# A tuned fp32 transformer trunk on one core: weight sums queued one split later, transposes moved behind the next block's first product, one filler step moved to the end of a block

## The chip, the cores and the metric

The kernel runs on one core of a Trainium2 chip. Its time is the device time of the whole program in microseconds; the time before is the median of three runs. All instructions are written out in a flat program without loops on the chip. A scheduler orders each engine's queue when the program is built: every instruction has the priority of its place in the traced Python code, and an instruction of lower priority is put first where the one ahead of it is not ready by the scheduler's own estimate. At run time each engine works through its queue strictly in order and waits on semaphores.

## The reference, cut to what matters

Two layers over x of 256 rows by 2048 columns, all in float32. Layer 0 has a gated linear attention mixer and layer 1 a sparse attention mixer; the change touches neither. After each mixer comes the same feed-forward part, with D_FF = 5632:

```
def swiglu(h, w1, w3, w2):
    return (jax.nn.silu(h @ w1) * (h @ w3)) @ w2
...
        x = x + y
        x = x + swiglu(rmsnorm(x, norm_ffn[i]), ffn_w1[i], ffn_w3[i], ffn_w2[i])
```

## The kernel before

**Split weights.** TensorE works on a reduced-precision form of float32, so each operand is split in two. A weight tile of 512 x 512 (1 MB, as 128 partitions x 2048 elements) is loaded by DMA, ScalarE casts it to its high part `wh` (L136), and VectorE subtracts to get the low part `wl` (L137). Each product is then three matmuls: high x high, high x low, low x high. Both `wh` and `wl` have three buffers, so a split can begin only when TensorE has finished with the tile that was split three splits earlier. Tiles that arrive for one use only go to four `raw` buffers.

**Blocks.** `ffn` (L561) goes over D_FF in units of 512 columns. `plain` does unit 0. Then come seven blocks per layer (L594), fourteen in all. Each block computes its own unit of `h @ w1` and `h @ w3` together in `pair` (L369), as a 2 x 2 block product done with seven products in place of eight. Below they are p1 to p7, by their forms A11, F5, F3, A12, F6, F7, N22; each takes two weight tiles and 24 matmuls. The seven products need sums of weight tiles:

- `va` and `vb` are loaded into fixed homes, `vc` and `vd` into `raw` buffers.
- p1 uses `va`; right after each of its two splits VectorE adds `vb` to that half of `va` (`plus`, L405, the instruction at L406). p2 uses the sum.
- After p2's splits the GpSimd queue starts a DMA that adds a tile from memory to `va` (`plus_dma`, L408 and L409). The second half's DMA is issued when the first half's has landed. p5 uses the result.
- p3 uses `vc`, and VectorE adds `vc` to `vb` (L406 again). A `raw` buffer of `vc` is free for its next load when this sum is done. p6 uses `vb`.
- After p5's splits two more DMAs of L409 add a tile to `va`, again one after the other; p7 uses that.

**Filler steps.** Wherever `pair` yields, `ffn` runs one step of other work: eight steps to a block, s0 to s7, each with one `raw` weight tile and 24 matmuls. In four of the seven blocks of a layer the work is `pieces` (L538), the down projection of two finished units: its matmuls are L551 to L553, its tile in PSUM is `down`, and after every second step VectorE adds two PSUM tiles to x (L558). In the first, the fourth and the last block it is `plain_steps` (L477), a further unit of `h @ w1` and `h @ w3` (matmuls L494, tile `half`). The order on TensorE is

```
p1 s0 p2 s1 p3 s2 p4 s3 p5 s4 p6 s5 s6 p7 s7 | p1 s0 ...
```

**Transposes.** When a block's unit is done it has to be transposed and split (`split_t`, L209, or `turned` in `plain_steps`, L515): eight transposes on TensorE, two casts on ScalarE (L218 or L528), two subtractions on VectorE (L219 or L529). These are generators in the deque `side`; `tick` (L116) runs one step of the first of them, and a product or a filler step ticks after every second of its k tiles. So they fall into p1 of the next block; behind a block with `plain_steps` there are two units to turn, and they fill p1 wholly.

Of the kernel before, what the change touches and what calls it, by code (L numbers as in the profile page):

```python
# [55 lines left out]
def trunk(  # L56
# [7 lines left out]
    nc = tc.nc  # L64
# [47 lines left out]


    side = deque()

    def tick():  # L116

        while side:
            try:
                return next(side[0])  # L120
            except StopIteration:
                side.popleft()
# [9 lines left out]
    def split_w(raw, pool=wp):  # L132

        wh = pool.tile([P, 4, NB], F32R, tag="wh", bufs=3 if pool is wp else 1, name="wh")
        wl = pool.tile([P, 4, NB], F32R, tag="wl", bufs=3 if pool is wp else 1, name="wl")
        nc.scalar.copy(wh, raw)  # L136
        nc.vector.tensor_sub(wl, raw, wh.bitcast(F32))  # L137
        return wh, wl

    def gemm_tail(w, c0, parts, pool, done):  # L140
# [228 lines left out]
    def pair(nrm, wa, wb, c0, turn, done):  # L369

        def src(w, j, c):
            r = j * 1024 + c * 512
            return w[r:r + 512, c0:c0 + NB].rearrange("(k p) n -> p k n", p=P)

        def load(w, j, homes):
            o = []
            for c, (pool, tag, bufs) in enumerate(homes):
                raw = pool.tile([P, 4, NB], F32, tag=tag, bufs=bufs, name=tag)  # L380
                nc.sync.dma_start(raw, src(w, j, c))
                o.append(raw)
            return o

        def product(acc, raws, form, start, stop, then=None):
            for c in range(2):
                wh, wl = split_w(raws[c])
                if then is not None:
                    then(c)
                hi, lo = nrm.forms[form]  # L390
                for j in range(4):
                    k = 4 * c + j
                    for i, (l_, r_) in enumerate(((hi, wh), (hi, wl), (lo, wh))):
                        nc.tensor.matmul(acc, l_[:, k, :], r_[:, j, :], start=start and k == i == 0,  # L394
                                         stop=stop and k == 7 and i == 2, skip_group_check=not start)
                    if j % 2:
                        tick()

        def bank():
            return acc_p.tile([P, NB], F32, tag="acc", name="acc")  # L400

        def sums(tag):
            return nrm.pool.tile([P, NB], F32, tag=tag, bufs=1, name=tag)

        def plus(dst, other):  # L405
            return lambda c: nc.vector.tensor_add(dst[c], dst[c], other[c])  # L406

        def plus_dma(dst, w, j):  # L408
            return lambda c: nc.gpsimd.dma_start(dst[c], src(w, j, c), accum_op=ALU.add)  # L409

        fz = nrm.pool
        stream = [(wp, "raw", RAW)] * 2
        homes = [((fz, "v0", 1), (fz, "v1", 1)), ((fz, "v2", 1), (res, "g3", 1))]
        va = load(wa, 0, homes[turn])
        vb = load(wb, 0, homes[1 - turn])
        b1 = bank()
        product(b1, va, "A11", True, True, plus(va, vb))
        s1 = sums("s1")
        nc.scalar.copy(s1, b1)
        yield  # L420
        b2 = bank()
        product(b2, va, "F5", True, True, plus_dma(va, wb, 1))
        y = sums("y")
        nc.vector.tensor_sub(y, b2, s1)
        yield
        vc = load(wb, 1, stream)
        product(b2, vc, "F3", False, True, plus(vb, vc))
        yield
        vd = load(wa, 1, stream)
        product(b1, vd, "A12", False, True)  # L430
        done("11", b1)
        yield
        b3 = bank()
        product(b3, va, "F6", True, True, plus_dma(va, wa, 1))
        w = sums("w")
        nc.vector.tensor_sub(w, b3, s1)
        nc.vector.tensor_add(w, w, b2)
        done("12", w)
        yield
        product(b3, vb, "F7", False, True)  # L440
        nc.vector.tensor_add(y, y, b3)
        yield
        yield
        product(b3, va, "N22", False, True)
        nc.vector.tensor_sub(s1, s1, b3)
        done("21", s1)
        done("22", y)
        yield

    def plain(nrm, ws, c0, done):  # L450
# [26 lines left out]
    def plain_steps(ws, b, forms, sc, ready):  # L477

        flat = res.tile([P, 4 * NB], F32, tag=f"g{b % 3}", name="early")
        us = [flat[:, t * NB:(t + 1) * NB] for t in range(NT)]  # L480
        s1 = flat[:, NT * NB:(NT + 1) * NB]
        for q, w in enumerate(ws):
            acc = [ms_p.tile([P, NB], F32, tag="ms", name="half") for _ in range(2)]
            for gi in range(4):
                raw = wp.tile([P, 4, NB], F32, tag="raw", bufs=RAW, name="raw")
                nc.sync.dma_start(raw, w[gi * NB:(gi + 1) * NB, b * NB:(b + 1) * NB].rearrange("(k p) n -> p k n", p=P))
                wh, wl = split_w(raw)
                for bank, form, start, stop in ((0, "A11", True, True), (1, "F7", True, True)) if gi < 2 else \
                        ((0, "A12", False, True), (1, "N22", True, True)):
                    hi, lo = forms[form]  # L490
                    for j in range(4):
                        k = 4 * (gi % 2) + j
                        for i, (l_, r_) in enumerate(((hi, wh), (hi, wl), (lo, wh))):
                            nc.tensor.matmul(acc[bank], l_[:, k, :], r_[:, j, :], start=start and k == i == 0,  # L494
                                             stop=stop and k == 7 and i == 2, skip_group_check=not start)
                        if j % 2:
                            tick()
                if gi == 1:
                    nc.scalar.copy(s1, acc[0])
                    nc.vector.tensor_add(s1, s1, acc[1])  # L500
                    acc[1] = ms_p.tile([P, NB], F32, tag="ms", name="half")
                if gi < 3:
                    yield
            r = sc["r"]
            if q == 0:
                nc.scalar.activation(us[0], acc[0], AF.Silu, scale=r[:, 0:1])
                nc.vector.tensor_sub(s1, s1, acc[1])
                nc.scalar.activation(us[1], s1, AF.Silu, scale=r[:, 1:2])
                yield
            else:  # L510
                nc.vector.scalar_tensor_tensor(us[0], us[0], r[:, 0:1], acc[0], op0=ALU.mult, op1=ALU.mult)
                nc.vector.tensor_sub(s1, s1, acc[1])
                nc.vector.scalar_tensor_tensor(us[1], us[1], r[:, 1:2], s1, op0=ALU.mult, op1=ALU.mult)

        def turned():  # L515
            tr = []
            for kk in range(2):
                tr.append(tr_p.tile([P, 2, SEQ], F32, tag="tr", name="tr"))
                for t in range(NT):
                    for k in range(2):  # L520
                        c = (2 * kk + k) * P
                        nc.tensor.transpose(tr[kk][:, k, t * P:(t + 1) * P], us[t][:, c:c + P], ident)
                if kk == 0:
                    yield
            hi, lo = hi_lo(b % 3)
            for kk in range(2):
                sl = slice(2 * kk, 2 * kk + 2)
                nc.scalar.copy(hi[:, sl, :], tr[kk])  # L528
                nc.vector.tensor_sub(lo[:, sl, :], tr[kk], hi[:, sl, :].bitcast(F32))  # L529
            part[:2] = hi, lo  # L530
            ready.add(b * NB)
            yield

        part = [None, None, b * NB]
        side.append(turned())
        yield part

    def pieces(w, parts):  # L538

# [21 lines left out]
    def ffn(layer, nrm):  # L561
# [2 lines left out]
        sc = {}  # L564
        parts = []
        ready = set()

        def block(b, us):
            def turned():
                yield from split_t(us, hi, lo)  # L570
                ready.add(b * NB)

            hi, lo = hi_lo(b % 3)
            side.append(turned())
            parts.append((hi, lo, b * NB))

        def gate(us):
# [16 lines left out]
        for turn, (b, inner) in enumerate(((2, 1), (3, None), (4, None), (6, 5), (7, None), (8, None), (10, 9))):  # L594
# [5 lines left out]
            us = [None] * NT  # L600
            made = None
            for slot, _ in enumerate(pair(nrm, w1, w3, b * NB, 1 - turn % 2, gate(us))):
                if inner is None and slot == 0:
                    assert all(r0 in ready for _, _, r0 in two)
                made = next(work)
            if inner is not None:
                parts.append(made)
            block(b, us)
        return w2, parts


# [554 lines left out]
```

## Time and profile before

| | us |
|---|---|
| median of 3 runs | 2260.61 (2259.99 to 2260.88) |
| profiled execution, its own time | 2262.72 |
| its span, first to last instruction | 2260.9 |
| TensorE busy | 2226.0 (98%) |
| VectorE busy | 1576.4 (70%) |
| ScalarE busy | 1169.4 (52%) |
| mean granted TensorE clock | 0.999 |

PE is TensorE, PEld its weight load, DVE VectorE, ACT ScalarE, POOL GpSimd and SPq the DMA queue of SyncE. TensorE's busy time counts pipelined matmuls, whose records overlap by 0.16 us: the starts of two matmuls with 512 columns are 0.23 us apart, while one record lasts 0.39 us. So an idle time that is shown is shorter than the delay between starts.

### The profile page before, as it was taken

Reading aid. Unit: us, or ns where it says so; the run is one execution under the profiler, and the core shown is the slowest. Engines: PE = TensorE matmul, PEld = TensorE weight load, DVE = VectorE, ACT = ScalarE, POOL = GpSimd, SP = SyncE. Lnnn points to the kernel's source line nnn. Section 1 sums busy time; section 2 is a strip of 40 time slices with the busy share of each in tenths; the row PEclk is TensorE's granted clock in tenths of the full one; section 3 lists DMA queues with packets and bytes.
Section 4 is the critical chain, followed back from the end, with each engine's and each line's share of the span. In section 5 each row is a group of like instructions: output and inputs, shape, how many; then the busy total and the mean of one; then the engine's idle time right before and its main releaser. Section 6 shows DMA issues by size and latency. Waiting matters only on the chain.

```text
span 2260.9 us, 25126 instructions
## 1 busy us (share of the span) xinstructions
PE 2226.0 (98%) x10247; PEld 1834.7 (81%) x10247; DVE 1576.4 (70%) x1282; ACT 1169.4 (52%) x1046; POOL 100.1 (4%) x147
## 2 busy tenths in 40 slices
PE   9999999999999999999999999999999999999998
PEld 8888888887787887788888888888888778778787
DVE  6546455778878888876555755556887886887874
ACT  5545455555555555555444544555554555555553
POOL 0000000000000000000100000000000000000000
PEclk9999999999999999999999999999999999999999
DMA  8555465597797797795554555457779779779763
GB/s 289 169 170 188 128 229 184 200 290 223 231 290 219 233 276 228 230 264 179 176 181 150 185 169 168 160 194 242 200 212 313 212 217 310 213 219 304 222 203 111
DMA packets 250547, 484.96 MB, mean 214 GB/s; under 512 B 8072, under 2 KB 20704, under 8 KB 250304
## 3 DMA queue, kind: packets, MB, share of 16 engines
q1 hardware_dynamic: 219856, 423.33, 54.3%
q0 software_dynamic: 29568, 58.72, 15.0%
q8 instruction: 80, 1.31, 0.2%
q10 hardware_dynamic: 1008, 1.31, 0.2%
q14 instruction: 35, 0.29, 0.0%
HBM read 481.20 MB, written 2.12 MB: 214 GB/s over the span
## 4 chain that ended last, share of the span: by engine, by line
PE 81%; DVE 11%; DMA 3%; ACT 2%; issue 2%; SPq 0%; POOL 0%; POOLq 0%; ACTq 0%
PE acc L394 15%; PE acc L202 12%; PE acc L204 12%; PE acc L203 12%; PE half L494 9%; DVE wl L137 4%; PE down L552 4%; PE down L553 4%; PE down L551 4%; DMA raw<-in_ffn_w 3%; PE acc L464 3%; DVE v L406 2%; ACT wh L136 2%; DVE g L406 1%; DVE x L558 1%
## 5 line engine op out<-in xcount | busy, mean ns | idle before, releaser
L136 ACT CAST wh<-raw 128x2048 fp32r<-128x2048 f32 x187 | 358.0, 1915 | 439.4 <-PE down L553 164.3
L137 DVE TENSOR_TENSOR wl<-raw,wh 128x2048 fp32r<-128x2048 f32 x187 | 426.8, 2289 | 204.1 <-ACT wh L136 203.9
L193 DVE TENSOR_TENSOR wl<-raw,wh 128x2048 fp32r<-128x2048 f32 (+3 forms) x161 | 349.9, 2176 | 302.2 <-ACT wh L192 302.1
L192 ACT CAST wh<-raw 128x2048 fp32r<-128x2048 f32 (+3 forms) x161 | 291.9, 1816 | 261.5 <-PE acc L204 211.0
L202 PE MATMUL acc<-wh,hh 128*128 128x512 f32 (+3 forms) x832 | 325.5, 391 | 0.0
L204 PE MATMUL acc<-wh,hl 128*128 128x512 f32 (+3 forms) x832 | 317.3, 381 | 0.0
L203 PE MATMUL acc<-wl,hh 128*128 128x512 f32 (+3 forms) x832 | 316.3, 380 | 0.6 <-DVE wl L193 0.6
L137 DVE TENSOR_TENSOR wl<-v,wh 128x2048 fp32r<-128x2048 f32 x102 | 232.8, 2287 | 24.5 <-ACT wh L136 24.4
L136 ACT CAST wh<-v 128x2048 fp32r<-128x2048 f32 x102 | 195.2, 1913 | 76.6 <-PE acc L394 43.4
L552 PE MATMUL down<-wl,g 128*128 128x512 f32 x512 | 201.3, 393 | 13.7 <-DVE wl L137 13.5
L553 PE MATMUL down<-wh,g 128*128 128x512 f32 x512 | 199.6, 390 | 0.0
L551 PE MATMUL down<-wh,g 128*128 128x512 f32 x512 | 198.3, 391 | 0.0
L203 PEld LDWEIGHTS acc<-wl,hh 128*128 128x128 f32 x832 | 156.7, 188 | 29.5 <-issue 1.7
L204 PEld LDWEIGHTS acc<-wh,hl 128*128 128x128 f32 x832 | 156.3, 188 | 29.5
L202 PEld LDWEIGHTS acc<-wh,hh 128*128 128x128 f32 x832 | 156.5, 188 | 28.6 <-issue 1.9
L394 PE MATMUL acc<-wh,fhF 128*128 128x512 f32 x448 | 174.6, 390 | 0.0
L394 PE MATMUL acc<-wl,fhF 128*128 128x512 f32 x448 | 174.3, 389 | 0.0
L394 PE MATMUL acc<-wh,flF 128*128 128x512 f32 x448 | 174.3, 389 | 0.0
L202 PE MATMUL acc<-wh,g 128*128 128x512 f32 x424 | 167.0, 394 | 0.0
L203 PE MATMUL acc<-wl,g 128*128 128x512 f32 x424 | 165.8, 391 | 0.0
L204 PE MATMUL acc<-wh,g 128*128 128x512 f32 x424 | 165.6, 391 | 0.0
L552 PEld LDWEIGHTS down<-wl,g 128*128 128x128 f32 x512 | 96.1, 188 | 39.2 <-DVE wl L137 20.2
(311 smaller groups left out, 3608.5 us busy)
## 6 DMA issues: line engine op xcount, KB each, us to landing
raw<-in_ffn_w SPq DMA_DIRECT2D x208, 1024.0 KB, 7.0
raw<-in_dsa_w_in SPq DMA_DIRECT2D x48, 1024.0 KB, 5.0
v<-in_ffn_w SPq DMA_DIRECT2D x42, 1024.0 KB, 8.4
raw<-in_gla_w_in SPq DMA_DIRECT2D x40, 1024.0 KB, 5.1
v<-in_ffn_w POOLq DMA_DIRECT2D x40, 1024.0 KB, 9.0
raw<-in_gla_w_out SPq DMA_DIRECT2D x16, 1024.0 KB, 5.0
g<-in_ffn_w POOLq DMA_DIRECT2D x16, 1024.0 KB, 13.0
raw<-in_dsa_w_out SPq DMA_DIRECT2D x16, 1024.0 KB, 4.9
```

The costliest lines, as they stand in the source:

```text
L136: nc.scalar.copy(wh, raw)
L137: nc.vector.tensor_sub(wl, raw, wh.bitcast(F32))
L192: a = nc.scalar.copy(wh[:, sl, :n], raw[:, sl, :n])
L193: v = nc.vector.tensor_sub(wl[:, sl, :n], raw[:, sl, :n], wh[:, sl, :n].bitcast(F32))
L202: nc.tensor.matmul(acc[t][:, :n], hi[:, k, ts_], wh[:, k, :n], start=start, stop=False)
L203: nc.tensor.matmul(acc[t][:, :n], hi[:, k, ts_], wl[:, k, :n], start=False, stop=False)
L204: nc.tensor.matmul(acc[t][:, :n], lo[:, k, ts_], wh[:, k, :n], start=False, stop=last)
L394: nc.tensor.matmul(acc, l_[:, k, :], r_[:, j, :], start=start and k == i == 0, stop=stop and k == 7 and i == 2, skip_group_check=not start)
L494: nc.tensor.matmul(acc[bank], l_[:, k, :], r_[:, j, :], start=start and k == i == 0, stop=stop and k == 7 and i == 2, skip_group_check=not ...
L551: nc.tensor.matmul(acc[t], hi[:, k, ts_], wh[:, k, :], start=start, stop=False)
L552: nc.tensor.matmul(acc[t], hi[:, k, ts_], wl[:, k, :], start=False, stop=False)
L553: nc.tensor.matmul(acc[t], lo[:, k, ts_], wh[:, k, :], start=False, stop=last)
```

## The change

VectorE's two kinds of weight sums (`plus`, at p1 and at p3) are no longer traced right after the split of their own half, but put into a deque; `split_w` takes one from it after the next split, whichever product or step that belongs to. The units that are to be transposed go into a list `late`, and come into `side` when the next block's p1 has been traced, so that s0 and p2 tick them. And p7 comes in front of s6, which now stands behind it:

```
p1 s0 p2 s1 p3 s2 p4 s3 p5 s4 p6 s5 p7 s6 s7 | p1 s0 ...
```

```diff
+    sums_due = deque()
...
         nc.scalar.copy(wh, raw)
         nc.vector.tensor_sub(wl, raw, wh.bitcast(F32))
+        if sums_due:
+            sums_due.popleft()()
         return wh, wl
...
         def plus(dst, other):
-            return lambda c: nc.vector.tensor_add(dst[c], dst[c], other[c])
+
+            return lambda c: sums_due.append(lambda: nc.vector.tensor_add(dst[c], dst[c], other[c]))
...
         product(b3, vb, "F7", False, True)
         nc.vector.tensor_add(y, y, b3)
         yield
-        yield
         product(b3, va, "N22", False, True)
         nc.vector.tensor_sub(s1, s1, b3)
         done("21", s1)
         done("22", y)
+        yield
         yield
...
         part = [None, None, b * NB]
-        side.append(turned())
-        yield part
+        yield part, turned()
...
+        late = []
...
             hi, lo = hi_lo(b % 3)
-            side.append(turned())
+            late.append(turned())
             parts.append((hi, lo, b * NB))
...
             for slot, _ in enumerate(pair(nrm, w1, w3, b * NB, 1 - turn % 2, gate(us))):
-                if inner is None and slot == 0:
-                    assert all(r0 in ready for _, _, r0 in two)
+                if slot == 0:
+                    side.extend(late)
+                    late.clear()
+                if inner is None and slot < 2:
+                    assert two[slot][2] in ready
                 made = next(work)
             if inner is not None:
-                parts.append(made)
+                parts.append(made[0])
+                late.append(made[1])
             block(b, us)
+        side.extend(late)
         return w2, parts
```

## Rows read from the trace of the kernel before

**Rows 1.** Page, part 1: busy time of each engine.

```profile
PE 2226.0 (98%) x10247; PEld 1834.7 (81%) x10247; DVE 1576.4 (70%) x1282; ACT 1169.4 (52%) x1046; POOL 100.1 (4%) x147
```

**Rows 2.** Waits of TensorE: who, for whom, total us, times, longest.

```profile
PE down L552 <- DVE wl L137: 13.5, 12, 1.6
PE half L494 <- DVE wl L137: 7.3, 6, 1.6
```

**Rows 3.** Timeline of TensorE, 614.2 to 617.2: start, length, instruction, idle before.

```profile
614.34 0.61 PE L551 MATMUL down<-wh,g 128*128 128x512 f32 x2
614.80 0.39 PE L394 MATMUL acc<-wh,fhF 128*128 128x512 f32 x1
616.77 0.50 PE L552 MATMUL down<-wl,g 128*128 128x512 f32 x1 [1.58 <-DVE wl L137]
617.11 0.40 PE L553 MATMUL down<-wh,g 128*128 128x512 f32 x1
```

**Rows 4.** Timeline of VectorE, 601.9 to 623, s7 and the next block's p1, s0.

```profile
604.16 0.68 DVE L445 TENSOR_TENSOR s<-s,acc 128x512 f32<-128x512 f32 x1
604.76 2.28 DVE L406 TENSOR_TENSOR v<-v,v 128x2048 f32<-128x2048 f32 x1
606.96 0.74 DVE L584 SCALAR_TENSOR_TENSOR u<-u,rstd,y 128x512 f32<-128x512 f32 x1
607.62 1.27 DVE L558 TENSOR_TENSOR x<-x,down 128x512 f32<-128x512 f32 x2
608.82 2.28 DVE L137 TENSOR_TENSOR wl<-g,wh 128x2048 fp32r<-128x2048 f32 x1
611.02 0.68 DVE L219 TENSOR_TENSOR g<-tr,g 128x512 fp32r<-128x512 f32 x1
611.62 2.28 DVE L406 TENSOR_TENSOR g<-g,v 128x2048 f32<-128x2048 f32 x1
...
614.43 2.28 DVE L137 TENSOR_TENSOR wl<-raw,wh 128x2048 fp32r<-128x2048 f32 x1
...
621.04 2.28 DVE L406 TENSOR_TENSOR v<-v,raw 128x2048 f32<-128x2048 f32 x1
```

**Rows 5.** Timeline of ScalarE, 601.9 to 623, the cast for s1.

```profile
622.17 1.92 ACT L136 CAST wh<-raw 128x2048 fp32r<-128x2048 f32 x1 [5.19 <-PE down L553]
```

**Rows 6.** Timeline of TensorE, 784.9 to 787.7, behind a block with `plain_steps`.

```profile
787.28 0.50 PE L552 MATMUL down<-wl,g 128*128 128x512 f32 x1 [1.36 <-DVE wl L137]
```

**Rows 7.** Timeline of TensorE, 591.1 to 592.2, between s5 and s6.

```profile
591.46 0.39 PE L394 MATMUL acc<-wh,fhN 128*128 128x512 f32 x1
591.73 0.50 PE L551 MATMUL down<-wh,g 128*128 128x512 f32 x1
592.06 0.40 PE L552 MATMUL down<-wl,g 128*128 128x512 f32 x1
```

**Rows 8.** Line L409 over the whole span; one DMA of it: landing, start.

```profile
DMA to landing us min/median/max: 8.5/9.7/15.6
...
v<-in_ffn_w POOLq DMA_DIRECT2D x1, 1024.0 KB, 14.7
...
1898.15 1.30 POOL L409 DMA_DIRECT2D v<-in_ffn_w  x1 [8.50 <-issue]
```

**Rows 9.** Timeline of TensorE, 1907.5 to 1914: s6 begins.

```profile
1913.43 0.39 PE L494 MATMUL half<-wh,fhA 128*128 128x512 f32 x1
```

**Rows 10.** Windows of one block: length, busy us of each engine, clock, DMA share, GB/s.

```profile
633.00:685.00 52.00, 52.00 (x230) 42.74 (x229) 36.34 (x24) 27.41 (x16) 2.59 (x2) 1.00 1.03 318
685.00:699.00 14.00, 14.00 (x67) 11.62 (x66) 13.79 (x11) 9.32 (x7) 0.00 (x0) 1.00 0.26 84
```

**Rows 11.** Block from 785: VectorE's sum, ScalarE's cast, TensorE's wait at s3.

```profile
803.86 2.29 DVE L406 TENSOR_TENSOR v<-v,raw 128x2048 f32<-128x2048 f32 x1
...
816.13 1.91 ACT L136 CAST wh<-raw 128x2048 fp32r<-128x2048 f32 x1 [3.52 <-DMA raw<-in_ffn_w]
...
820.42 0.50 PE L552 MATMUL down<-wl,g 128*128 128x512 f32 x1 [0.66 <-DVE wl L137]
```

## The prediction

> **What bounds the kernel now.** I read the page's busy times first [rows 1]: TensorE is busy for 98% of the span, VectorE for 70%. Only TensorE's own waits can then be won back, some 35 us in all, and the table of its waits says for whom [rows 2]: 20.8 us in 18 waits for `wl`, VectorE's low half of a weight tile, the longest 1.6 us each time, all at filler steps (L552 and L494). Next I laid the timelines of TensorE, VectorE and ScalarE beside each other around these waits. Twelve of the 18 stand in one place: at s0, behind the first product of a block, at each of the six borders between blocks in each layer. Eight idle 1.58 to 1.59 us there [rows 3]; the four behind a block with `plain_steps` 1.36 to 1.39 [rows 6]. Together that is 18.2 us; the other 2.6 are six short waits at s3.
>
> VectorE's timeline shows why [rows 4]. From 604.16 to 616.7 it has no gap: the end of p7 (0.68 and 0.74), the x adds of s7 (1.27), the split of p1's second half (2.28), both weight sums of p1 (2.28 each), the transposes' two subtractions (0.68 each), and only then s0's split, which starts at 614.43. TensorE comes to s0 at 614.34, so it waits until the split is done at 616.7. That VectorE is idle for 30% of the span does not help here.
>
> What a wait costs is more than its idle time. Starts are 0.23 us apart in steady work; here L552 starts 1.97 behind the matmul before it, and L553 0.34 behind that [rows 3]: 1.74 + 0.11 = 1.85 us. At the four other borders the last transpose would give way after 0.2 us, and 1.36 idle makes 1.5 us by the same count [rows 6].
>
> **The change part by part.** *The border.* Three edits take work from before s0's split. The second sum goes behind it by priority (2.28 us); the two subtractions go to s0's own ticks (1.36, or 2.7 where two units are turned); p7's end comes one filler step earlier, 5.44 us (24 x 0.2267), so its 0.68 and 0.74 fall into s6 (1.42). That is 5.1 us against a lateness of 1.6. To see what is late next I lay out the new order with no wait, t = 0 at the start of s6. A split takes a cast of 1.92 on ScalarE [rows 5] and 2.28 on VectorE; it begins when TensorE leaves the tile split three splits before, as in [rows 5], where s1's cast waits for s0's last matmul.
>
> - s6 runs from 0 to 5.4, s7 to 10.9, p1 to 16.3, s0 with its eight transposes (0.7) to 22.5, p2 to 27.9, s1 to 33.3.
> - p1's first split: cast 0.2 to 2.1, low half to 4.4; then p7's 0.74 to 5.1, and the first sum until 7.4, while the second half's cast (5.6 to 7.6) runs. Second low half 7.6 to 9.9. VectorE is then idle, so the second sum fits from 9.9 to 12.2, then the x adds to 13.6.
> - s0's cast is 11.1 to 13.0, its low half 13.6 to 15.9. TensorE wants it at 16.8, behind two high-half matmuls: 0.9 us to spare. Behind `plain_steps`, with three operations of about 0.7 in place of the x adds, it ends at 16.6: 0.2 to spare.
> - p2's halves: 15.9 to 18.2, and by 23.5, wanted at 22.7 and 25.4.
>
> So all twelve waits go: 8 x 1.85 + 4 x 1.5 = **-20.8 us**. The spare time is worked out with other work in its way only once, so what may stay at s0 is bounded by 0 and one operation of 0.7 at each border, 8.4; I take 0.2 at the four tight ones, **+0.8**, since the eight others have room for it.
>
> *p7 in front of s6.* First a small gain. Today s6 needs the PSUM tiles that s5's x adds have still to read, so one matmul of p7 is put between and s6 starts 0.27 and 0.33 later instead of 0.23 [rows 7]: 0.15 us. With p7 between them the x adds are done. Eight blocks have this form (`pieces` at s6 as well as s5): **-1.2**, or 0 if the scheduler mixes them again.
>
> Then the price. s6's 24 matmuls stood between s5 and p7, and they cover a transfer: the second DMA of p5's pair, which adds to the half of `va` that p7 uses second. In the tightest block it starts at 1898.15 and lands 14.7 us later, at 1912.85 [rows 8]. Cast and low half end at 1917.1. p7 would start where s6 starts now, 1913.43 [rows 9], and want that low half 2.72 + 0.23 later, at 1916.4: 0.7 us late, where today it has 4.7 us to spare. The same working in the fourteen blocks gives from 5.5 us of spare to 0.8 of lateness, and lateness in two, 1.0 us in all. If VectorE's x adds after s5 (1.27, [rows 4]) or the copy of `plain_steps` stand first, seven blocks are late, 5.6 us in all. I take **+3.0**, between the two, since the trace does not show which order the queue will take. s6 moved also means its own cast, split and `raw` buffer come one product later: the load that its buffer waits for (the next `vc`) starts 5 us later but is wanted five steps on. The loads of `vb`, queued on SP behind p7's splits, start 5 us earlier; they take the place that the `vc` load had in SP's queue, so the DMA of p5's pair sees the same company.
>
> The Trainium skill, "DMA: Bandwidth & Descriptors", section "Issuing engines are not separate DMA queues", says that transfers issued by SyncE, ScalarE and GpSimd share the same 16 engines and interleave. The trace agrees: the same 1 MB from GpSimd lands after 8.5 to 15.6 us [rows 8]. By that rule nothing protects p7's transfer from SP's loads, which is the second rival below; by the row alone the sum stays as it is.
>
> *The sums of p3.* They too are traced one split later, the second behind s2's split. The queue need not follow: in the old trace p3's first sum already stands at 621.04, before s1's split, because ScalarE's cast for s1 had to wait until 622.17 [rows 4, 5]. The same gap stays. I take 0; the ends are -2.6 (the six waits at s3 [rows 2] vanish, as VectorE comes to p3 less pressed) and what the first rival says.
>
> Sum: -20.8 + 0.8 - 1.2 + 3.0 + 0 = -18.2 us. On the profiled span that is 2260.9 - 18.2 = 2242.7, with the 1.8 us around it 2244.5 of the profiled execution's 2262.72. The median of the runs is 2260.61, 2.1 below that: **2242.5**. Its own range: the best ends give -20.8 - 1.2 + 1.0 - 2.6 = -23.6, the worst -20.8 + 8.4 + 5.6 = -6.8, but all of the worst at once is unlikely; 2237 to 2250.
>
> **The rivals.**
>
> *Slower: `vc`'s buffer comes free too late.* A `raw` buffer is loaded again only when p3's second sum has read it. In the block from 785 that sum ended at 806.15, the load landed in time for a cast at 816.13, and TensorE still waited 0.66 us at s3 [rows 11]. Were the sum to stand behind s2's split, as traced, that split would end at 807.5, the sum at 809.8: 3.7 us later, with the load and the wait following. In twelve blocks that is up to 44 us against 22 won: some 2280. It decides from 22 / 12 = 1.8 us a block. For it: mid-block the load has no slack. Against it: s2's cast cannot start before s1's matmuls end, VectorE has 1.9 us without a split there, and the queue took sums early before.
>
> *p7's transfer takes the gain back in part.* If it lands 2 us later, nine of fourteen blocks are late, 12 us in all, with the operations ahead some 15: 2260.6 - 22.0 + 15 = 2254. At 3.0 us later, a little less than 1 MB takes at the 318 GB/s of [rows 10], all 22 are eaten.
>
> *No change: the transfers set the pace.* In the block's middle the DMA share is 1.03 for 52 us [rows 10]; what TensorE wins at s0 could be waited for at s3, time 2260 within 2. Against it: the first load of that stretch is released by s0's split itself, which comes 1 us earlier against TensorE than now, and the share falls to 0.26 around the border. The Trainium skill, "Perfetto Trace Analysis", section "Roofline", gives a single core some 435 GB/s over its 16 engines; by that ceiling the stretch at 318 would not be full, and its 16.5 MB would take 38 us (an estimate), which makes this rival weaker than the row does.
>
> **How the numbers follow.** The forecast has 0.76, p7's transfer 0.12, no change 0.06, the slower rival 0.06. About 0.2%, 4.5 us, is what can be told from no change. The first two cases are faster by more than that: 0.88; same 0.06; slower 0.06. The range for 8 in 10 takes in the forecast's own and the second rival: 2236 to 2254.
>
> **What would show it.** Right: TensorE's waits for `wl` at s0 are gone from the table of waits, its total under 8 us; the sum at L406 stands behind s0's split or in a gap before it; L219 and L529 come after s0's split; p7's matmuls follow s5's directly. Wrong: a new wait of L394 (N22) for `wl` over 1 us in most blocks (p7's transfer); waits at s3 above 2 us with the cast released by a `raw` DMA (the slower rival); or the old wait at s0 still 1 us or more because other work has moved in front of its split.

## The result and the profile after

The changed kernel takes **2234.1 us**, the median of four runs (2232.6 to 2237.1). The kernel before, run beside it on the same chip, takes 2260.5 (2260.0 to 2260.9). The ratio is 0.9885 with a 95% interval of 0.9868 to 0.9902: 26.4 us or 1.2% faster. The forecast was 2242.5 with a range of 2236 to 2254, so the direction was right, and the time lies 1.9 us below the range. The profiled execution took 2233.9 us with a span of 2232.1; the span before was 2260.9, so the two traces differ by 28.8 us.

The busy times, to be set beside [rows 1]:

```profile
PE 2217.3 (99%) x10247; PEld 1837.9 (82%) x10247; DVE 1577.6 (71%) x1282; ACT 1172.2 (53%) x1046; POOL 100.1 (4%) x147
```

Every engine has as many instructions as before, and VectorE's busy time is the same within 1.2 us. No work went away; waits did. TensorE's table of waits, which answers to [rows 2] (who, for whom, total us, times, longest):

```profile
PE trc L110 <- DMA rows<-in_norm_mix: 4.3, 1, 4.3
PE acc L206 <- DVE wl L196: 0.6, 1, 0.6
PE trki L958 <- DVE kin L884: 0.6, 1, 0.6
PE acc L397 <- DVE wl L138: 0.6, 1, 0.6
```

The two lines that led [rows 2], 20.8 us in 18 waits, are gone. The first three lines here lie outside the fourteen blocks and were there before. The fourth is new: one wait of 0.56 us at p7, in one block of fourteen.

The border that [rows 3] and [rows 4] showed looks like this in TensorE's timeline (L554 to L556 are the three matmuls of `pieces`, L551 to L553 before; L397 is `product`):

```profile
610.67 0.39 PE L397 MATMUL acc<-wh,flA 128*128 128x512 f32 x1
610.89 0.39 PE L554 MATMUL down<-wh,g 128*128 128x512 f32 x1
611.12 0.39 PE L555 MATMUL down<-wl,g 128*128 128x512 f32 x1
```

The matmul that takes s0's `wl` now starts 0.23 us behind the one before it, where it stood 1.97 behind in [rows 3]. VectorE's timeline shows what moved (L138 is a split's low half, L410 a weight sum, L448 and L588 the end of p7, L561 the x adds, L222 the transposes' subtractions):

```profile
596.21 0.68 DVE L448 TENSOR_TENSOR s<-s,acc 128x512 f32<-128x512 f32 x1
596.81 2.28 DVE L138 TENSOR_TENSOR wl<-v,wh 128x2048 fp32r<-128x2048 f32 x1
599.01 0.74 DVE L588 SCALAR_TENSOR_TENSOR u<-u,rstd,y 128x512 f32<-128x512 f32 x1
599.67 2.28 DVE L410 TENSOR_TENSOR v<-v,v 128x2048 f32<-128x2048 f32 x1
601.99 2.29 DVE L410 TENSOR_TENSOR v<-v,raw 128x2048 f32<-128x2048 f32 x1
604.20 2.29 DVE L138 TENSOR_TENSOR wl<-g,wh 128x2048 fp32r<-128x2048 f32 x1
606.40 1.28 DVE L561 TENSOR_TENSOR x<-x,down 128x512 f32<-128x512 f32 x2
607.65 2.29 DVE L138 TENSOR_TENSOR wl<-raw,wh 128x2048 fp32r<-128x2048 f32 x1
609.86 2.29 DVE L410 TENSOR_TENSOR g<-g,v 128x2048 f32<-128x2048 f32 x1
...
616.46 0.68 DVE L222 TENSOR_TENSOR g<-tr,g 128x512 fp32r<-128x512 f32 x1
617.06 2.28 DVE L410 TENSOR_TENSOR v<-v,raw 128x2048 f32<-128x2048 f32 x1
```

VectorE is still without a gap here. But s0's split (607.65 to 609.9) now ends a microsecond before s0 starts at 610.89; in [rows 4] it ended 2.4 us after TensorE had come. The second sum of p1 (609.86) and the transposes' subtraction (616.46) now stand behind this split, and p7's subtraction (596.21) stands ahead of p1's first split (596.81). One thing is not in the working of the prediction: p3's first sum, at 621.04 before, behind p2's splits, now runs at 601.99, before p1's second split. The time that the prediction had given to p1's second sum went to it, and p1's second sum came behind s0's split.

To count what all waits cost I use the measure of the prediction, not idle time: over every start of TensorE in the fourteen blocks, what exceeds the regular spacing, added up by the step at which it falls. Before it is 29.2 us: 21.1 at s0, 4.6 at s3, 2.5 at s1, 0.9 at s6, 0.2 at p4. After it is 2.0: 0.84 at p7, 0.54 at transposes, 0.42 at s0, 0.22 at s6. That explains 27.2 of the 28.8 us; where the other 1.6 lie was not followed.

### The profile page after: what moved, and what is told of

Its sections match the earlier page's. It is cut to its first block, busy times and chain, and to the rows that moved or that the text cites. A ratio compares the mean times of both kernels' runs of the same rounds, so it can differ in the third digit from the quotient of the medians.

```text
span 2232.1 us, 25168 instructions
## 1 busy us (share of the span) xinstructions
PE 2217.3 (99%) x10247; PEld 1837.9 (82%) x10247; DVE 1577.6 (71%) x1282; ACT 1172.2 (53%) x1046; POOL 100.1 (4%) x147
## 4 chain that ended last, share of the span: by engine, by line
PE 94%; DVE 2%; issue 1%; ACT 1%; DMA 1%; POOL 0%; POOLq 0%; ACTq 0%; DVEq 0%
PE acc L397 23%; PE acc L205 12%; PE acc L207 12%; PE acc L206 12%; PE half L498 11%; PE down L555 5%; PE down L556 5%; PE down L554 5%; PE acc L468 3%; PE tr L219 1%; DVE wl L138 1%; DMA g<-in_ffn_w 1%; PE trq L906 0%; PE po L765 0%; PE tr L253 0%
## 5 line engine op out<-in xcount | busy, mean ns | idle before, releaser
L138 DVE TENSOR_TENSOR wl<-raw,wh 128x2048 fp32r<-128x2048 f32 x187 | 427.1, 2289 | 160.2 <-ACT wh L137 159.9
L138 DVE TENSOR_TENSOR wl<-v,wh 128x2048 fp32r<-128x2048 f32 x102 | 232.8, 2288 | 34.2 <-ACT wh L137 34.1
L554 PE MATMUL down<-wh,g 128*128 128x512 f32 x512 | 200.0, 391 | 0.0
L556 PE MATMUL down<-wh,g 128*128 128x512 f32 x512 | 199.4, 389 | 0.0
L397 PE MATMUL acc<-wh,fhF 128*128 128x512 f32 x448 | 175.1, 391 | 0.0
L397 PE MATMUL acc<-wh,flF 128*128 128x512 f32 x448 | 174.8, 390 | 0.0
L397 PE MATMUL acc<-wl,fhF 128*128 128x512 f32 x448 | 174.7, 390 | 0.0
```

Of the source, the lines that this page charges most:

```text
L554: nc.tensor.matmul(acc[t], hi[:, k, ts_], wh[:, k, :], start=start, stop=False)
L556: nc.tensor.matmul(acc[t], lo[:, k, ts_], wh[:, k, :], start=False, stop=last)
```

## The experiments

The prediction counted 20.8 us at s0 and left the waits at s1 and s3 as they were. They went too, 7.2 us with the 0.2 at p4. Two theories of why: **A**, they are VectorE's backlog from the border, and p7's end, moved ahead, is what clears it; **B**, at least those at s3 are waits for transfers, and what decides is when s3's load lands. The delays below are counted as above, each from its own kernel's trace.

**One edit alone.** Three kernels are the one before with one edit each: `sums_only` has the queue `sums_due`, `late_only` the list `late`, `p7_only` the moved `yield`.

```diff
 # sums_only: the kernel before, with
         nc.vector.tensor_sub(wl, raw, wh.bitcast(F32))
+        if sums_due:
+            sums_due.popleft()()
 ...
-            return lambda c: nc.vector.tensor_add(dst[c], dst[c], other[c])
+            return lambda c: sums_due.append(lambda: nc.vector.tensor_add(dst[c], dst[c], other[c]))
```

```diff
 # late_only: the kernel before, with
-            side.append(turned())
+            late.append(turned())
 ...
-                if inner is None and slot == 0:
-                    assert all(r0 in ready for _, _, r0 in two)
+                if slot == 0:
+                    side.extend(late)
+                    late.clear()
+                if inner is None and slot < 2:
+                    assert two[slot][2] in ready
```

```diff
 # p7_only: the kernel before, with
         yield
-        yield
         product(b3, va, "N22", False, True)
 ...
+        yield
         yield
```

> The kernel before with the weight sums queued one split later, nothing else. Theory A (the waits at s1 and s3 are the tail of the same VectorE backlog, and only p7 in front of s6 lets VectorE run ahead of it): the second sum of 2.28 us leaves the place in front of s0's split, so the waits of 1.36 to 1.59 us at the border go, but VectorE has the same work to do before s1 with TensorE 1.85 us earlier, so waits at s1 and s3 stay or grow; gain 12 to 19 us, 2241 to 2248, TensorE's waits for wl 3 to 8 us. Theory B (the waits at s1 and s3 hang on the transfers, and go as soon as s0's split frees its buffer earlier): s1 and s3 go too, 2233 to 2238.

> The kernel before with the transposed units moved behind the next block's p1, nothing else. Two subtractions (1.36 us, 2.7 behind plain_steps) leave the place in front of s0's split. Theory A: the border keeps about 0.3 us at eight borders, s1 and s3 keep their waits; gain 10 to 16 us, 2244 to 2250. Theory B: s3's waits go as well, 2236 to 2241.

> The kernel before with p7 in front of s6, nothing else. Theory A: in s6 and s7 TensorE asks VectorE for one split per 5.4 us, VectorE gets ahead and takes p1's and one of p3's sums there; the border and the waits at s1 and s3 go with this edit alone, gain 23 to 28 us, 2232 to 2238. Theory B: the border's wait goes (1.42 us of p7's work and 0.2 more), s3 as well; the same range, so this run alone does not part them, but a gain under 20 us would speak against A.

`no_p7` is the changed kernel with that `yield` put back, so sums and turns only:

```diff
         nc.vector.tensor_add(y, y, b3)
         yield
+        yield
         product(b3, va, "N22", False, True)
 ...
-        yield
         yield
```

> The changed kernel with p7 back behind s6: sums and transposes moved. 3.6 us and more are taken from in front of s0's split. Theory A: border waits all gone, waits at s1 and s3 stay, gain 16 to 21 us, 2239 to 2245. Theory B: everything gone as in the changed kernel, 2232 to 2237.

Measured together on one chip, beside 2261.3 for the kernel before:

| kernel | median us | ratio, 95% | delays in the blocks, us |
|---|---|---|---|
| sums_only | 2242.8 | 0.9902 to 0.9931 | 9.6: s3 8.7, s6 0.9 |
| late_only | 2240.8 | 0.9891 to 0.9924 | 8.9: s0 6.4, s6 0.9, s3 0.8, others 0.8 |
| p7_only | 2240.0 | 0.9889 to 0.9918 | 7.0: s0 5.1, s6 0.7, p7 0.6, s3 0.4 |
| no_p7 | 2234.5 | 0.9866 to 0.9895 | 2.3: s6 0.9, p4 0.5, s1 0.4, s0 0.3, s3 0.3 |

Each edit alone wins 18.5 to 21.3 us, 60 in sum, and all three together 26.4. They relieve the same backlog. `sums_only` came out where A had put it; `late_only` won more than A's 16, `p7_only` less than A's 23, and `no_p7` fell into B's range. A's second half falls: `no_p7` gets nearly the whole gain without p7's move, and `late_only` won 20.6. Its first half holds for s1: 2.5 us before, nothing in `sums_only` and `p7_only`, 0.4 in the other two. For s3 these times decide nothing. A had its waits stay or grow in `sums_only`, and they grew, from 4.6 to 8.7 us, though VectorE is relieved enough that nothing is left at s0. What parts the theories at s3 is what its cast waits for, and the run with fewer bytes below. The table of waits of `sums_only`:

```profile
PE down L555 <- DVE wl L138: 4.7, 5, 1.6
PE half L497 <- DVE wl L138: 0.7, 2, 0.6
```

**One edit undone.** `no_late` is the changed kernel without `late` (sums and p7), `no_sums` without `sums_due` (turns and p7):

```diff
 # no_sums: the changed kernel, with
-            return lambda c: sums_due.append(lambda: nc.vector.tensor_add(dst[c], dst[c], other[c]))
+            return lambda c: nc.vector.tensor_add(dst[c], dst[c], other[c])
```

```diff
 # no_late: the changed kernel, with
-            late.append(turned())
+            side.append(turned())
```

> The changed kernel with the transposed units back in p1: sums and p7's place changed. Theory A: as fast as the changed kernel, 2232 to 2237. If each of the three edits is needed for the last waits: 2238 to 2244.

> The changed kernel with the weight sums back behind their own split: transposes and p7's place changed. Theory A: as fast as the changed kernel, 2232 to 2237. If each of the three edits is needed: 2238 to 2244.

Beside 2260.5 for the kernel before, `no_late` takes 2239.4 (0.9893 to 0.9923; s3 1.5, p7 0.9, s6 0.7, s1 0.7), and `no_sums` 2234.4 (0.9871 to 0.9900; s0 4.1, p7 0.6). So any two edits that include `late` give 26 us, sums and p7 together only 21. The runs of `no_late` spread from 2237.1 to 2242.9, and its delays are read from the fastest.

**The first rival, forced.** In the changed kernel the queue takes p3's sums long before the place where they are traced. `p3_pinned` ties each of them behind the split that it is traced behind:

```diff
-        nc.vector.tensor_sub(wl, raw, wh.bitcast(F32))
+        v = nc.vector.tensor_sub(wl, raw, wh.bitcast(F32))
         if sums_due:
-            sums_due.popleft()()
+            pinned, add = sums_due.popleft()
+            with behind((v.ins,) if pinned else None):
+                add()
 ...
-        product(b2, vc, "F3", False, True, plus(vb, vc))
+        product(b2, vc, "F3", False, True, plus(vb, vc, True))
```

> The changed kernel with p3's two sums bound in VectorE's queue behind the split at which they are traced (the second half of vc, and s2's tile). This is the first rival of the prediction made true. By it vc's buffers come free about 5 and 7 us later and the loads of vd's second half and of s3 with them; in the changed kernel s3's low half is ready only some 0.5 us before it is wanted, so waits of 3 to 7 us at s3 or p4 in twelve blocks: 2265 to 2310. If the loads have slack after all: under 2240.

It takes 2242.1 (0.9901 to 0.9931), 8.0 more than the changed kernel, between the two forecasts and not the 44 more that the rival gave. VectorE's timeline shows that the pin holds; p3's sums are at 629.37 and 634.97, each right behind a split:

```profile
627.17 2.28 DVE L138 TENSOR_TENSOR wl<-raw,wh 128x2048 fp32r<-128x2048 f32 x1
629.37 2.28 DVE L412 TENSOR_TENSOR v<-v,raw 128x2048 f32<-128x2048 f32 x1
631.57 1.28 DVE L563 TENSOR_TENSOR x<-x,down 128x512 f32<-128x512 f32 x2
632.77 2.29 DVE L138 TENSOR_TENSOR wl<-raw,wh 128x2048 fp32r<-128x2048 f32 x1
634.97 2.29 DVE L412 TENSOR_TENSOR v<-v,raw 128x2048 f32<-128x2048 f32 x1
```

Yet the delay at s3 is 0.45 us, over all fourteen blocks together. SP's queue says why. s3's load is issued at 635.08, as the split at 632.77 ends: it goes into the buffer that this split frees, and does not wait for the sum that ends at 637.26. In the third block of `p3_pinned`, SP's timeline:

```profile
635.08 0.37 SPq L549 DMA_DIRECT2D raw<-in_ffn_w  x1
```

and that DMA in the view of the DMAs (KB each, us to landing):

```profile
raw<-in_ffn_w SPq DMA_DIRECT2D x1, 1024.0 KB, 5.0
```

The same two lines of the changed kernel, first SP's timeline, then the DMA:

```profile
627.42 0.37 SPq L547 DMA_DIRECT2D raw<-in_ffn_w  x1
```

```profile
raw<-in_ffn_w SPq DMA_DIRECT2D x1, 1024.0 KB, 12.6
```

s3 starts at 646.69 in the one and at 644.52 in the other. So the pinned kernel issues this load 11.6 us before s3 instead of 17.1, and it lands 6.6 before s3 instead of 4.5: issued later, and landed earlier. Over the fourteen blocks it lands 0.5 us later on average (table below). What the pin costs lies elsewhere, 5.7 us at p7 and 2.5 at s6; why was not followed.

The pin does not make the whole rival true. In the kernel before, s3's load did wait for p3's second sum in four of the fourteen blocks. In the one of [rows 11] that sum ends at 806.15, and SP's timeline has

```profile
806.21 0.37 SPq L544 DMA_DIRECT2D raw<-in_ffn_w  x1
```

In the changed kernel that sum runs early, and a split releases the load in all fourteen blocks. In `p3_pinned` the load got another buffer. So what is tested is a load that starts 5.4 us later, not a load that waits for the sum. In this block of `p3_pinned` it is s4's load that waited for the sum: it was issued at 637.29 and landed after 5.4 us. That is 4.05 us before s3 starts, about in time for s3 as well (an estimate, by the 4.1 us below).

**Fewer bytes.** `sums_only` with one transfer of 1 MB left out in each block, the second half of p2's pair of accumulating DMAs:

```diff
-        product(b2, va, "F5", True, True, plus_dma(va, wb, 1))
+        add = plus_dma(va, wb, 1)
+        product(b2, va, "F5", True, True, lambda c: add(c) if c == 0 else None)
```

> The kernel with the weight sums alone moved, and in each block p2's second DMA that adds to va left out, so that half of va lacks one addend and 1 MB less is moved in a block's middle. In the run with the sums alone the waits at s3 had grown from 4.6 to 8.7 us. Theory B (the waits at s3 are transfers queued behind one another since the border): 1 MB, 3.3 us at 318 GB/s, goes from in front of s3's load, its waits fall under 2 us, 2233 to 2237. Theory A (VectorE's late sums and splits): the order and the work on VectorE are as they were, s3 keeps 6 us or more, 2240 to 2243.

It takes 2234.7 (0.9870 to 0.9899), 8.1 less than `sums_only`, and the delay at s3 is zero in all blocks. The second block of both, as ScalarE's cast for s3, first in `sums_only`:

```profile
559.05 1.92 ACT L137 CAST wh<-raw 128x2048 fp32r<-128x2048 f32 x1 [5.95 <-DMA raw<-in_ffn_w]
```

then in the kernel with 1 MB less:

```profile
556.76 1.91 ACT L137 CAST wh<-raw 128x2048 fp32r<-128x2048 f32 x1 [3.52 <-DVE wl L138]
```

In the first the cast waits for the load; s3 starts at 561.86, and its second matmul then waits 1.09 us. In the second the load has landed at 554.9, and the cast waits for something else, by the profile a split of VectorE. Both kernels issue this load 11.9 us before s3; it takes 8.9 us in the one and 4.8 in the other. So B holds for s3 this far: in `sums_only` the wait is for the load, and less traffic ahead of the load removes it with VectorE's order as it was. The transfer left out was an accumulating one; whether 1 MB of a plain load weighs as much was not tried. Over the fourteen blocks (the cast follows the landing by 0.1 us and the low half ends 4.24 after the cast's start, so a load that lands less than some 4.1 us before s3 is late):

| kernel | issued before s3, mean (least) | us to landing, median | landed before s3, mean (least) | delay at s3, us |
|---|---|---|---|---|
| before | 15.6 (13.2) | 11.2 | 4.3 (3.4) | 4.6 |
| after | 16.9 (16.3) | 11.9 | 5.4 (4.5) | 0 |
| sums_only | 13.6 (11.9) | 9.6 | 3.7 (2.4) | 8.7 |
| no_late | 16.9 (16.5) | 12.7 | 4.4 (3.6) | 1.5 |
| no_p7 | 13.7 (11.8) | 8.5 | 5.0 (4.0) | 0.3 |
| p3_pinned | 11.5 (11.0) | 6.8 | 4.9 (4.0) | 0.45 |
| sums_no_p2second | 13.6 (11.9) | 5.0 | 8.3 (6.9) | 0 |

When the load is issued and when it lands before s3 have little to do with each other. `no_late` issues as early as the changed kernel and lands a microsecond later; `p3_pinned` issues 5.4 us later and lands half a microsecond later. 1 MB less brings the landing forward by 4.6 us at the same times of issue. The time of issue itself hangs on VectorE and on p7's place. With p7 behind s6, p3's second sum releases this load in 4 blocks of the kernel before, 8 of `sums_only`, 8 of `no_p7` and 12 of `late_only`; with p7 moved, in none. Yet `no_p7` loses 0.3 us at s3 and `no_late`, with p7 moved, 1.5.

**p7's transfer.** `no_second` is the changed kernel without the second DMA of p5's pair, the one that p7 waits for; it shows what the transfer costs:

```diff
-        product(b3, va, "F6", True, True, plus_dma(va, wa, 1))
+        add = plus_dma(va, wa, 1)
+        product(b3, va, "F6", True, True, lambda c: add(c) if c == 0 else None)
```

`p7_earlier` goes on in the direction of the change and moves p7 ahead of s5 too:

```diff
         product(b3, vb, "F7", False, True)
         nc.vector.tensor_add(y, y, b3)
-        yield
         product(b3, va, "N22", False, True)
 ...
+        yield
         yield
         yield
```

> The changed kernel with p7 one filler step earlier still, right behind p6, and s5, s6, s7 behind it. The second DMA of p5's pair then is wanted 5.44 us earlier. If it is that transfer which bounds p7, its spare time in the changed kernel's trace (0.1 to 5.2 us in the fourteen blocks) turns into lateness of 0.2 to 5.3 us, some 40 us in all, less what later slack takes back: 2255 to 2275, with waits of L397 for wl or for the DMA at p7. If the transfer had room: 2230 to 2240.

> The changed kernel with the second DMA of p5's pair left out in each block, so that half of va lacks one addend and p7's second half waits for no transfer. If the spread of the changed kernel's runs (2232.6 to 2237.1) and its last wait at p7 come from that transfer: 2231 to 2233.5 with a spread under 1 us. If not: 2234 and the same spread.

`p7_earlier` takes 2338.7 (1.0324 to 1.0359): 105 us more than the changed kernel, 7.5 a block, for one step, and 64 above the range expected. TensorE waits 66 us at s5, for ScalarE's casts:

```profile
PE down L554 <- ACT wh L137: 37.8, 8, 6.7
PE half L498 <- ACT wh L137: 28.1, 6, 7.4
```

ScalarE's timeline in the first block:

```profile
494.81 1.91 ACT L137 CAST wh<-v 128x2048 fp32r<-128x2048 f32 x1 [3.47 <-PE half L498]
500.75 1.90 ACT L137 CAST wh<-g 128x2048 fp32r<-128x2048 f32 x1 [4.03 <-DMA g<-in_ffn_w]
502.55 1.89 ACT L137 CAST wh<-raw 128x2048 fp32r<-128x2048 f32 x1
```

p7's second cast waits 4.03 us for its transfer, and the cast for s5, whose data need nothing of that transfer, stands behind it in the same queue. p7's first half is ready by then; its low half ends at 499.04 in VectorE's timeline:

```profile
496.75 2.29 DVE L138 TENSOR_TENSOR wl<-v,wh 128x2048 fp32r<-128x2048 f32 x1 [1.63 <-ACT wh L137]
```

But two matmuls of s5 stand in front of it in TensorE's queue, in all fourteen blocks, so TensorE stands still until s5's cast is done. What follows on TensorE:

```profile
499.82 0.39 PE L397 MATMUL acc<-wh,flF 128*128 128x512 f32 x1
504.50 0.79 PE L498 MATMUL half<-wh,fhA 128*128 128x512 f32 x1 [4.29 <-ACT wh L137]
...
505.62 0.79 PE L397 MATMUL acc<-wh,fhN 128*128 128x512 f32 x1
506.21 0.63 PE L397 MATMUL acc<-wl,fhN 128*128 128x512 f32 x1
506.64 0.63 PE L397 MATMUL acc<-wh,flN 128*128 128x512 f32 x1
507.07 0.63 PE L397 MATMUL acc<-wh,fhN 128*128 128x512 f32 x1
```

Behind the wait starts are 0.43 us apart instead of 0.23. The windows of the two stretches (length, busy us of each engine, granted clock, DMA share, GB/s) give the granted clock as 0.98 and 0.53:

```profile
500.00:504.50 4.50, 0.21 (x2) 0.00 (x1) 1.82 (x1) 3.70 (x2) 0.00 (x0) 0.98 1.05 405
504.50:508.00 3.50, 3.50 (x8) 2.45 (x9) 3.27 (x3) 0.00 (x0) 0.00 (x0) 0.53 0.97 312
```

That is close to TensorE's lower level, 1.2 of 2.4 GHz, right behind 4.3 us without a matmul. By the count of delays the waits at s5 cost 72 us and the slow first half of p7 another 31. So the 105 us are not the transfer's alone. The 12 matmuls of p7's first half, 2.7 us at 0.2267 each, could have run within each wait (an estimate); no run has p7 here without s5's two matmuls in front of it.

In the changed kernel s5 stands in front of p7 and covers the transfer. `no_second` takes 2232.7 (2232.4 to 2233.0), with delays of 0.7 us. Against the changed kernel's two medians that is 0.4 us less (the runs beside it, below, whose range takes these in) and 1.4 less (its first runs, not made beside these). So the transfer costs the changed kernel 1.4 us at most; the 0.4 seen side by side is not clear of the spread.

**p7's move in the whole.** The changed kernel and `no_p7` once more, side by side in five rounds.

> The changed kernel itself, to be compared with the next run on the same chip: 2232 to 2236, spread of 3 us and more.

> The changed kernel with p7 back behind s6, again: 2234 to 2235.5, spread under 1.5 us. If p7's new place gives something of its own, the run before this one is faster by 1 us or more; if not, the two medians lie within 1 us.

The changed kernel takes 2233.0 (2232.3 to 2234.0; ratio 0.9859 to 0.9892) and `no_p7` 2234.8 (2234.6 to 2235.2; 0.9870 to 0.9900): 1.8 us for p7's move, with no run of the one within the range of the other. The changed kernel's runs spread by 1.7 us and not by the 3 expected. The first runs of the two kernels differ by 0.4 us, but they were not made side by side and their ranges overlap, so the size is not settled. No kernel that does the whole work was faster than the changed one.

## Why the prediction was wrong in its sum, though right about the border

The forecast was 8.4 us too slow, and the time lies below its range. (Its terms add up to 2242.4; the 0.1 is rounding.) The border's mechanism held. The step that failed is the term for p3's sums, put at 0.

**The border: right.** All twelve waits at s0 went, for the reason given. The term was -20.8 + 0.8 = -20.0; the count of delays gives 21.1 to 0.4, -20.7. The layout of s6 to s1 held in its times: s0's split was to end 0.9 us before it is wanted and ends 1.2 before (609.94 against 611.12). It did not hold in its order: p3's first sum ran in the time laid out for p1's second. Both take 2.3 us. That s0's split came out as laid out is thus in part luck. The chance of 0.76 lay on the right mechanism, and the signs in the profile were the ones named.

**s6: right, smaller.** -1.2 was forecast, and 0.9 to 0.2 measured, -0.7.

**p7's transfer: right in kind, too dear.** +3.0 was forecast, with one or more blocks late. One block is late in each of the two profiles of the changed kernel: 0.84 us in the first, 1.47 in the second. In the first it is block 8 of 14. Its DMA, in GpSimd's timeline and in the view of the DMAs (KB each, us to landing):

```profile
1626.60 1.29 POOL L413 DMA_DIRECT2D g<-in_ffn_w  x1 [8.59 <-issue]
```

```profile
g<-in_ffn_w POOLq DMA_DIRECT2D x1, 1024.0 KB, 14.5
```

The cast waits for it, the low half ends at 1645.41, and p7's second half has its first low-half matmul late. The timelines of ScalarE and VectorE, then of TensorE:

```profile
1641.18 1.91 ACT L137 CAST wh<-g 128x2048 fp32r<-128x2048 f32 x1 [5.43 <-DMA g<-in_ffn_w]
...
1643.12 2.29 DVE L138 TENSOR_TENSOR wl<-g,wh 128x2048 fp32r<-128x2048 f32 x1 [4.45 <-ACT wh L137]
```

```profile
1644.52 0.39 PE L397 MATMUL acc<-wh,fhN 128*128 128x512 f32 x1
1645.47 0.50 PE L397 MATMUL acc<-wl,fhN 128*128 128x512 f32 x1 [0.56 <-DVE wl L138]
```

In the other thirteen blocks the low half ends 0.5 to 3.9 us before it is wanted. The term is mis-sized because it took start and duration of each transfer from the old trace. The block of [rows 8], said to be 0.7 us late, now has its DMA start 16.1 us before p7 (15.3 in the forecast) and land after 12.4 us (14.7): 2.3 to spare. Over the fourteen blocks this DMA takes 11.9 us in the median; before, 12.9.

**The sums of p3: the step that failed.** The forecast took 0 with a best end of -2.6. The waits at s1 and s3 were worth 7.2 us (0.2 at p4 among them), and all of it went. Three faults lie in that step.

First, it said that the queue would leave p3's sums in the gap before s1's split. They moved up, from 621.04 and right behind it to 601.99 and 617.06. In the old order both stood in front of s1's split. The cast for s1 ends at 624.09 [rows 5], but VectorE is at the sums until 625.5. VectorE's timeline from 619 to 628.3, then TensorE's:

```profile
621.04 4.49 DVE L406 TENSOR_TENSOR v<-v,raw 128x2048 f32<-128x2048 f32 x2
625.44 2.28 DVE L137 TENSOR_TENSOR wl<-raw,wh 128x2048 fp32r<-128x2048 f32 x1
```

```profile
627.14 0.61 PE L551 MATMUL down<-wh,g 128*128 128x512 f32 x2
627.78 0.50 PE L552 MATMUL down<-wl,g 128*128 128x512 f32 x1
```

The two matmuls at 627.14 start 0.23 apart, and the third starts 0.41 behind them, 0.18 late. With the 0.11 of the one after it that is 0.3 us in each of eight blocks, the 2.5 us at s1. In all eight both sums stand directly in front of s1's split; in the six other blocks one does, and s1 loses nothing. The prediction quoted the first of these sums and did not see it as a cause.

Second, -2.6 is the idle time of six waits at s3; the prediction itself had shown, at s0, that a wait costs more than its idle time, and did not apply it here. Counted by starts, s3 was 4.6, and the 2.5 at s1 has hardly an idle record at all.

Third, no reason was seen why s3's waits should go. They are waits for transfers: the landing moved from 4.3 to 5.4 us before s3 on average, and no block falls below the 4.1 that s3 needs. p3's sums may have a part here too. In the four blocks of the kernel before where the second sum released the load, which hold 2.4 of the 4.6 us, the landing moved from 3.7 to 6.3 us before s3; in the ten others from 4.5 to 5.1. How much of this is the earlier issue and how much other traffic was not parted.

With -7.2 in place of 0 and +0.8 in place of +3.0 the sum would have been 2260.6 - 20.0 - 1.2 + 0.8 - 7.2 = 2233.0, against 2234.1 measured.

**The rivals.** The first, slower by up to 44 us, did not come. It took s3's load to wait for p3's second sum, which was so in four blocks of the kernel before; in the changed kernel the queue takes that sum early (617.06), and the load does not wait for it. It also took the load to land as much later as it is issued later, and `p3_pinned` speaks against that: issued 5.4 us later, it lands 0.5 us later. The second, p7's transfer, takes back up to 1.4 us here. One step on the loss is 105, from the transfer and the order of the queues together. The third, transfers that set the pace, is real but partial. It is seen where the border is relieved without turning units later: in `sums_only` s3 takes back 4.1 of the 21.1 us won at s0. The window from 628.4 to 677 of the changed kernel has a DMA share of 1.04, as in [rows 10], so the middle of a block is as full as before. The Trainium skill, "Perfetto Trace Analysis", section "Roofline", gives some 435 GB/s as a single core's ceiling, by which that window, at 302 GB/s, would have room to spare; the run with 1 MB less speaks against that here, and the measurement decides. A share near 1 does not stand for one rate either: `p7_earlier` moved 405 GB/s over 4.5 us at 1.05. What the Trainium skill says in "DMA: Bandwidth & Descriptors", section "Issuing engines are not separate DMA queues", that transfers of different issuers run on the same engines, the same run bears out: the transfer left out was GpSimd's, and the load that landed 4.6 us sooner is SP's.

**What stays open.** Why the landing at s3 differs by a microsecond between kernels with like times of issue. Kernels with `late` land 4.9 to 5.5 us before s3 on average, those without 3.7 to 4.4, `p7_only` excepted with 5.3. Turning units behind p1 lengthens TensorE's stretch from the border to s3 by 0.7 us or 1.4, which has the right sign and size; it was not tested by itself. More buffers for raw weight tiles, which would test it from the other side, were not tried.

## What to carry to other kernels

When one engine's queue is overfull at a border, several edits relieve the same backlog: price them together, since alone each of the three here won 18 to 21 us and all of them 26. Count waits by the spacing of starts on the engine that sets the pace and not by its idle time, or small waits in other steps (7.2 us here) are left out of the sum. And before moving a consumer ahead of a filler step, find the transfer that the filler covers and how many microseconds it has to spare: here one step was free within 1.4 us and the next cost 105. Look at the queues as well: part of that 105 is work that was ready and stood behind two matmuls that were not.

## What was not expected of the hardware

In the middle of a block of these kernels, with a DMA share of 1.03 to 1.06, the time of issue hardly decides when 1 MB lands. The same load issued 16.9 or 11.5 us before it is wanted landed 5.4 or 4.9 us before (medians to landing 11.9 and 6.8 us). Where 1 MB of accumulating traffic was taken out ahead of it, it landed after 5.0 instead of 9.6.

In `p7_earlier` a wait of 4.3 us was followed by a granted clock of 0.53 for the next 3.5 us. Behind such waits the first half of p7 loses 31 us over fourteen blocks, beside the 72 of the waits themselves.

The same DMA in the same block (p5's second, block 8) took 14.5 us in one execution of the changed kernel and 12.4 in another. The changed kernel's runs spread by 4.5 and 1.7 us; without this DMA by 0.5, and with s6 in front of p7 by 0.7.
